# A four-layer decoder trunk on one core: the state-space layers' small matmuls in four quarters of the array, two copies pinned, fetches moved and one order rewritten

## The chip, the core and the metric

The kernel runs on one core of a Trainium2 chip. The metric is the device time of one execution in microseconds (us). A core has TensorE (PE in the profile, PEld for its weight loads), VectorE (DVE), ScalarE (ACT), GpSimd (POOL) and SyncE (SP), which run side by side and wait for one another by semaphores. SP, ACT and POOL also issue DMAs, each in its own order, so that an instruction waiting at the head of a queue holds up what stands behind it.

## What is computed

A decoder trunk of four layers over 256 positions with 1024 features. Each layer has a token mixer, an MLP with squared ReLU and a gated input per layer ("ple"). The mixers of layers 0 and 3 are S5, a diagonal complex state-space model; layer 1 has forgetting attention, layer 2 gated linear attention. The change touches S5 alone. Cut to what matters:

```python
u = xn @ w_in                                  # (256, 1024): 64 groups of 16 channels
ab = exp((lam_re + 1j * lam_im) * dt)          # per group, 64 states
x = einsum('bsgc,gnc->bsgn', u, bbar)          # into the states, complex
s = associative_scan(s_t = ab * s_(t-1) + x_t) # over time
y = real(einsum('bsgn,gcn->bsgc', s, c)) + d_skip * u
z1, z2 = split(gelu(y) @ w_glu)
out = (z1 * sigmoid(z2)) @ w_out
```

## The kernel before

The residual stream lies in SBUF as features by time, float32. Large matrix products split each float32 weight tile into a high and a low part (`parts`: ACT casts the high part, L182; DVE subtracts for the low part, L184) and run three matmuls per pair of tiles (L201 to L203, or `wide`, L237 and L239). S5's small products are plain float32 matmuls, each of which is two records in the trace.

S5 takes time in steps of four positions, so that one group has 4 x 16 = 64 inputs and outputs per step, 64 steps and 64 states. The 64 groups are worked in four blocks b of 16: eight pairs p, and in a pair the halves g = 0 (partitions 0 to 63) and g = 1 (64 to 127). One block goes through these steps, each a letter in an order string:

- w: projection `x @ w_in` in eight pieces, two per block (L1241); D: the DMA of a piece's weights on SP.
- u: scale by the norm, and eight small DMAs on SP and ACT that turn the block's inputs into U, 64 inputs by 64 steps per group (L1247, L1075).
- i, r, o, k (layer 0 only): DVE builds the weights into the states, the rotations, the weights out of them and the direct part tm (L968 to L993, L1008 to L1045). For layer 3 the same things are computed during earlier MLPs (`s5_ahead`) and kept in DRAM ("kept").
- f, q (in layer 3): fetch from DRAM, on POOL: f takes win (weights in) and rot, q the weights out and tm (L1215, L1052).
- x: `s5_way_in`, matmuls from U to the states (L1087), one per pair, half, and real or imaginary part, and twice that in layer 0, where each weight comes in two terms. Results lie in two PSUM tiles "wk", the real and the imaginary one.
- s: `s5_states` on DVE: rotation (L1097 to L1099) and the scan (L1102). e: `s5_turned`, rotation back (L1110 to L1121).
- y: `s5_outputs`, matmuls from U and the states to the outputs in one PSUM tile "mk" (L1133), then a GELU on ACT (L1142).
- t: four transposes on PE into the PSUM tile "po" (L1149) and a copy of the high part (L1150); g: its low part on DVE (L1313).
- a, b: gate products of w_glu's second half, one unit of a block's features each (L201 to L203); d: DMA of such a unit; l: its split. P, p: the ple projection's DMA and its pieces (L470).
- c, n, z: the norm.

In x and y each matmul has 64 rows by 64 columns of weights and 64 moving columns. Half g reads partitions of its half and writes partitions of the same half, so the two matmuls of a pair lie on the diagonal of the 128 x 128 array.

The order strings FIRST (layer 0) and LATER (layer 3) say in which order steps are written down. A scheduler then orders each engine's instructions, by that order and its own model of time; in layer 3 `in_order` holds PE to the written order. `issue_after(i)` puts an engine's instructions behind instruction i of the same engine. Tiles come from pools by tag, with as many buffers as BUFS says, and a tile waits until its buffer's last user is done. "win" has one buffer, shared with scratch of `s5_in`; "wt" has four, "po" and "mk" one each, "raw" three.

Of the kernel before, what the change touches and what calls it, by code (L numbers as in the profile page):

```python
# [22 lines left out]
        "acc": 3, "wk": 3, "po": 1, "mk": 1}  # L23
# [6 lines left out]
LATER = """D0 D2 D1 D3 c0 w0 w2 n0 z0 f0 q0 w1 z1 D4 D5 u0 w3 P0 u1 w4 D6 D7 d0 x0 s0 w5 d1 f1 q1 x1 e0 w6 y0 u2 s1 w7 t0 l0 g0 f2 x2 u3 P1 e1 q2 y1 l1 d2  # L30
s2 p0 p1 t1 g1 f3 x3 q3 p2 e2 y2 p3 d3 s3 a0 t2 g2 l2 d4 b0 l3 d5 a1 e3 l4 d6 b1 l5 d7 y3 a2 l6 t3 b2 l7 g3 a3 b3"""
# [29 lines left out]
class Trunk:  # L61
# [849 lines left out]
    def s5_table(self, j, F):  # L911

        nc = self.nc
        ps = self.psum((128, 2, 128), "mk")
        nc.tensor.matmul(ps.rearrange("p i x -> p (i x)"), self.zero[:, 0:128], self.zero[:, 0:256], start=True, stop=True)
        for i in range(2):
            nc.tensor.transpose(ps[:, i, :], F[:, i].rearrange("x s p -> x (s p)"), self.ident)
        ct = self.a2("ct", (128, 2, 2, 64))
        nc.scalar.copy(ct.rearrange("x i g n -> x i (g n)"), ps)
        self.ct = ct  # L920
        tab = self.dram.tile([2, 4, 4, 2, 8, 64], F32, name=f"tab{j}")
        for i in range(2):
            for g in range(2):
                nc.gpsimd.dma_start(tab[g, :, :, i].rearrange("s b p n -> (s b) p n"), ct[:, i, g, :])
        return tab

    def s5_spread(self, b):

        out = []
        for i in range(2):  # L930
            ps = self.psum()
            for p in range(8):
                for g in range(2):
                    self.last_mm = self.nc.tensor.matmul(ps[g * 64:(g + 1) * 64, p * 64:(p + 1) * 64], self.pick[:, p], self.ct[:, i, g, :], start=True, stop=True, skip_group_check=True)
            out.append(ps)
        return out
# [8 lines left out]
    def s5_fetch_in(self, j, b, pin=lambda x: x):  # L945
        bT = self.t4("bT", (128, 2, 512), tag="wt")
        pin(self.nc.gpsimd.dma_start(bT, self.A["s5_bT"][j, b]))
        return bT

    def s5_fetch_powers(self, tab, b, pin=lambda x: x):  # L950
        cf = self.t4("coef", (128, 2, 512), tag="wt")
        for g in range(2):
            pin(self.nc.gpsimd.dma_start(cf[g * 64:(g + 1) * 64], tab[g, :, b].rearrange("s i p n -> s (i p n)").unsqueeze(0).broadcast_to([16, 4, 1024])))
        return cf
# [6 lines left out]
    def s5_in(self, b, bT, cf, ahead=False):  # L961

        nc = self.nc
        if not ahead:
            w = [self.wp.tile([128, 2, 8, 64], F32, name=n, tag=n, bufs=BUFS[n]) for n in ("wh", "wl")]
            f = [t.rearrange("x i p n -> x i (p n)") for t in w]
            re, im = cf
            nc.vector.tensor_tensor(f[0], bT, re.unsqueeze(1).broadcast_to([128, 2, 512]), ALU.mult)  # L968
# [4 lines left out]
        w = [self.flat(win[:, i]) for i in range(2)]  # L973
        t = self.scratch((2, 512))
        t = [t[:, i] for i in range(2)]
        self.two(w[0], bT[:, 0], cf[:, 0], bT[:, 1], cf[:, 1], ALU.subtract, t[0])
        yield
        self.two(w[1], bT[:, 0], cf[:, 1], bT[:, 1], cf[:, 0], ALU.add, t[1])
        self.keep(b, 0, win, ahead)
# [97 lines left out]

    def s5_way_in(self, U, win):

        xs = []  # L1080
        for ri in range(2):
            px = self.psum((128, 8, 64))
            for p in range(8):
                for i, w in enumerate(win[ri]):
                    for g in range(2):
                        r = slice(g * 64, (g + 1) * 64)
                        self.nc.tensor.matmul(px[r, p, :], w[r, p], U[r, p, :], start=i == 0, stop=i == len(win[ri]) - 1, skip_group_check=True)  # L1087
            xs.append(px)
        return xs

    def s5_states(self, xs, rot, d0):
# [3 lines left out]
        X, Y = (t.rearrange("x i p j -> x (i p j)").rearrange("x (p i j) -> x p i j", p=8, i=2) for t in (P, W))  # L1095
        for t, px in zip((X, Y), xs):
            V.tensor_tensor(t, px.unsqueeze(2).broadcast_to([128, 8, 2, 64]), rot, ALU.mult)  # L1097
        V.tensor_tensor(R[:, 0], X[:, :, 1], Y[:, :, 0], ALU.add)
        V.tensor_tensor(R[:, 1], X[:, :, 0], Y[:, :, 1], ALU.subtract)  # L1099
# [24 lines left out]
    def s5_outputs(self, U, terms, out, tm):  # L1124
# [3 lines left out]
        py = self.psum((128, 8, 64), "mk")  # L1128
        gs = [slice(g * 64, (g + 1) * 64) for g in range(2)]
        def add(x, w, start=False, stop=False):  # L1130
            for p in range(8):
                for g in range(2):
                    nc.tensor.matmul(py[gs[g], p, :], x[gs[g], p, :], w[gs[g], :, p] if w is not tm else w[gs[g], p], start=start and p == 0,  # L1133
                                     stop=stop and p == 7, skip_group_check=True)


        add(U, tm, start=True)
        parts = [(t[n], out[i]) for n in range(len(terms[0])) for i, t in enumerate(terms)]
        for n, (t, w) in enumerate(parts):
            add(t, w, stop=n == len(parts) - 1)  # L1140
        G = self.t2("G", (128, 4, 8, 16))
        self.last_gelu = nc.scalar.activation(G, py.rearrange("x p (i c) -> x i p c", i=4), AF.Gelu_apprx_tanh)  # L1142
# [57 lines left out]
    def s5_start(self, l):  # L1200
# [100 lines left out]
        def e(b):  # L1301
            states[b] = self.s5_turned(*states[b], rots[b][0], first)
# [41 lines left out]
        steps = dict(D=D, w=w, u=u, c=c, n=n, z=z, f=f, j=j_, q=q_, r=r, i=i, o=o, k=k, x=x_, s=s, e=e, y=y, t=t, g=g, P=P, p=p, d=d, l=ahead, a=lambda b: gate(0, b),  # L1344
# [144 lines left out]
def layout(inputs):  # L1489
# [42 lines left out]
```

## Time and profile before

| | |
|---|---|
| median of 3 runs | 1417.9 us (1415.36 to 1418.76) |
| profiled execution | 1413.62 us, its span 1411.9 us |
| mean granted TensorE clock | 0.994 |
| layer 0's S5, x of block 0 to g of block 3 | 29.96 to 123.6 us |
| layer 3's S5, w of piece 0 to g of block 3 | 1058.03 to 1137.8 us |
| ACT busy over the span | 708.5 us (50%) |
| DMA | 254.80 MB, mean 180 GB/s |

The span runs from the first to the last instruction; the execution's own time lies a little around it. A row of the timeline has the start, the length, engine, line, operation, the tile written and those read, the shape and the count of merged records; in brackets how long the engine was idle before and what ended that. A row of busy time by stage has the window and its length, busy us and records of PE, PEld, DVE, ACT and POOL, the granted TensorE clock, the DMA share and GB/s.

### The profile page before, as it was taken

How to read it: one execution, taken by the hardware profiler on the slowest of the kernel's cores; microseconds unless marked ns; L12 is line 12 of the kernel's file. 1: busy time of each engine (PE TensorE's matmuls, PEld its weight loads, DVE VectorE, ACT ScalarE, POOL GpSimd, SP SyncE). 2: the span in 40 equal slices, each digit the busy share in tenths (PEclk: the TensorE clock that was granted, in tenths of full speed). 3: DMA queues.
4: the chain of work that ended last, by engine and by line, in shares of the span. 5: the costliest groups of instructions: out<-in, count | busy, mean ns of one | idle time of the engine just before them, and what ended most of it. 6: DMA issues, size and time to landing. Idle time of an engine off the chain costs nothing.

```text
span 1411.9 us, 26657 instructions
## 1 busy us (share of the span) xinstructions
PE 1376.1 (97%) x10794; PEld 1247.5 (88%) x10794; DVE 1034.7 (73%) x1638; ACT 708.5 (50%) x1110; POOL 107.7 (8%) x179
## 2 busy tenths in 40 slices
PE   9898999999999999999999999999999999999997
PEld 8788988889999978888988698888998899888897
DVE  9985678776867678897676568888666857766764
ACT  3234565454645565455566355555452355545553
POOL 3000000010110000110005100100004100000020
PEclk9999999999999999999999999999999999999999
DMA  9434656657554446776665356666666455556551
GB/s 306 128 114 124 182 176 196 184 182 234 181 149 138 133 136 209 249 232 206 183 187 148 107 162 195 212 206 220 203 207 204 164 195 172 187 167 212 188 180 60
DMA packets 144475, 254.80 MB, mean 180 GB/s; under 512 B 22192, under 2 KB 33552, under 8 KB 144352
## 3 DMA queue, kind: packets, MB, share of 16 engines
q1 hardware_dynamic: 130336, 227.80, 51.9%
q0 software_dynamic: 7744, 23.73, 4.9%
q10 hardware_dynamic: 6272, 1.58, 0.5%
q8 instruction: 84, 1.38, 0.4%
q14 instruction: 39, 0.32, 0.1%
HBM read 242.81 MB, written 8.13 MB: 178 GB/s over the span
## 4 chain that ended last, share of the span: by engine, by line
PE 65%; ACT 1%; DVE 1%; issue 1%; POOL 1%; DMA 1%; DVEq 0%; POOLq 0%; ACTq 0%; SPq 0%
PE wk L237 9%; PE acc L237 7%; PE wk L239 5%; PE acc L239 4%; PE acc L201 3%; PE wk L201 3%; PE wk L202 3%; PE wk L203 3%; PE acc L202 3%; PE acc L203 3%; PE mk L237 3%; PE po L237 2%; PE acc L1241 2%; PE mk L239 1%; PE acc L264 1%; PE acc L265 1%
## 5 line engine op out<-in xcount | busy, mean ns | idle before, releaser
L184 DVE TENSOR_TENSOR wlo<-raw,whi 128x1024 fp32r<-128x1024 f32 x396 | 482.5, 1226 | 270.5 <-ACT whi L182 266.2
L182 ACT CAST whi<-raw 128x1024 fp32r<-128x1024 f32 x396 | 412.5, 1049 | 484.3 <-PE po L237 73.8
L237 PE MATMUL wk<-x,whi 128*128 128x512 f32 x576 | 181.7, 396 | 0.8 <-DVE relu L248 0.8
L239 PEld LDWEIGHTS wk<-x,wlo 128*128 128x128 f32 x576 | 107.1, 188 | 23.6
L237 PE MATMUL acc<-s,whi 128*128 128x512 f32 x384 | 119.7, 395 | 0.0
L239 PE MATMUL wk<-x,wlo 128*128 128x256 f32 x576 | 113.4, 279 | 0.0
L237 PEld LDWEIGHTS wk<-x,whi 128*128 128x128 f32 x576 | 89.8, 189 | 2.5 <-DVE relu L248 0.8
L239 PEld LDWEIGHTS acc<-s,wlo 128*128 128x128 f32 x384 | 71.4, 188 | 16.5
L201 PE MATMUL acc<-x,whi 128*128 128x256 f32 x288 | 81.6, 287 | 0.9 <-ACT pp L456 0.9
L203 PE MATMUL acc<-x,wlo 128*128 128x256 f32 x288 | 82.1, 286 | 0.2 <-DVE wlo L184 0.2
L202 PE MATMUL acc<-x,whi 128*128 128x256 f32 x288 | 81.8, 285 | 0.0
L237 PE MATMUL mk<-x,whi 128*128 128x512 f32 x256 | 81.6, 395 | 0.0
L239 PE MATMUL acc<-s,wlo 128*128 128x256 f32 x384 | 76.0, 280 | 0.0
L203 PE MATMUL wk<-s,wlo 128*128 128x256 f32 x256 | 72.4, 283 | 0.0
L202 PE MATMUL wk<-s,whi 128*128 128x256 f32 x256 | 72.4, 283 | 0.0
L201 PE MATMUL wk<-s,whi 128*128 128x256 f32 x256 | 72.4, 283 | 0.0
L237 PE MATMUL po<-s,whi 128*128 128x512 f32 x192 | 60.3, 395 | 0.0
L237 PE MATMUL wk<-s,whi 128*128 128x512 f32 x192 | 59.5, 395 | 0.0
L237 PEld LDWEIGHTS acc<-s,whi 128*128 128x128 f32 x384 | 58.9, 189 | 0.6
L237 PE MATMUL acc<-x,whi 128*128 128x512 f32 x192 | 58.8, 396 | 0.0
L239 PEld LDWEIGHTS mk<-x,wlo 128*128 128x128 f32 x256 | 47.6, 188 | 10.3
L201 PEld LDWEIGHTS acc<-x,whi 128*128 128x128 f32 x288 | 54.7, 191 | 1.9 <-ACT pp L456 1.1
(413 smaller groups left out, 3382.6 us busy)
## 6 DMA issues: line engine op xcount, KB each, us to landing
raw<-mlp_w SPq DMA_DIRECT2D x256, 512.0 KB, 3.8
raw<-s_w_glu SPq DMA_DIRECT2D x32, 512.0 KB, 4.5
raw<-ple_gate SPq DMA_DIRECT2D x32, 512.0 KB, 3.6
raw<-fox_w_in SPq DMA_DIRECT2D x24, 512.0 KB, 3.8
raw<-gla_w_in SPq DMA_DIRECT2D x24, 512.0 KB, 3.7
raw<-s_w_out SPq DMA_DIRECT2D x16, 512.0 KB, 3.6
kept<-kept POOLq DMA_DIRECT2D x12, 512.0 KB, 5.3
raw<-ple_proj SPq DMA_DIRECT2D x8, 512.0 KB
```

Of the source, the lines that this page charges most:

```text
L182: nc.scalar.copy(hi, raw)
L184: self.last_lo = nc.vector.tensor_tensor(lo, raw, hi.bitcast(F32), ALU.subtract)
L201: mm(ps, hi, x[:, 0], start=first, stop=False, skip_group_check=True)
L202: mm(ps, hi, x[:, 1], start=False, stop=False, skip_group_check=True)
L203: self.last_mm = mm(ps, lo, x[:, 0], start=False, stop=last, skip_group_check=True)
L237: mm(ps[n], hi[:, i, s], v[i], start=first and i == 0, stop=False, skip_group_check=True)
L239: self.last_mm = mm(ps[n][:, 0], lo[:, i, s], v[i][:, 0], start=False, stop=last and i == UK - 1, skip_group_check=True)
L264: mm(ps[half], a[:, 0, t], hi[:, k], start=k0 + k == 0, stop=False)
L265: mm(ps[half], a[:, 0, t], lo[:, k], start=False, stop=False)
L1241: self.last_mm = nc.tensor.matmul(ps[:, n], raw[:, k, c], x[4 * i + k], start=i == k == n == 0, stop=i == 1 and k == 3, skip_group_check=True)
```

## The change

- In pairs p = 4 to 7 the two groups trade halves where states lie: the state of half g lies on partitions of half 1 - g. The host lays out lam, b, c and d so (`turned`), and the table of powers is stored by h = p // 4. With that a step of x or y has four matmuls in a row, h = 0 and 1 by g = 0 and 1, one in each 64 x 64 quarter of the array: those of h = 1 lie off the diagonal.
- x writes PSUM tiles by h, not by real and imaginary part; y writes two half-sized tiles, "mk" for h = 0 and "po" for h = 1. Matmuls are as many as before, of the same size.
- s works on one h at a time: two products of the old size, four adds of half the old size. The GELU comes in two halves.
- For y's direct term with h = 1 the inputs must lie on the other half of the partitions: `s5_inputs_turned` copies U's pairs 4 to 7 across, two ACT copies per block, in step e, and for b > 0 pinned behind the last GELU written down.
- Layer 3: win is fetched by a step of its own, F, into "wt", no longer by f into "win". The order LATER is new: F0 and F1 near the norm, F2 and F3 after w4; u2 ahead of e0; step v7 is w7 with t0 between its halves; x3 ahead of t1 and p1; a0 ahead of y2; p2, p3 after y2; g1 after y2, g2 after a1.
- Powers are fetched by four DMAs per block on POOL, not two.

```diff
+        "v1": 2, "acc": 3, "wk": 3, "po": 1, "mk": 1}
-LATER = """D0 D2 D1 D3 c0 w0 w2 n0 z0 f0 q0 w1 z1 D4 D5 u0 w3 P0 u1 w4 D6 D7 d0 x0 s0 w5 d1 f1 q1 x1 e0 w6 y0 u2 s1 w7 t0 l0 g0 f2 x2 u3 P1 e1 q2 y1 l1 d2
-s2 p0 p1 t1 g1 f3 x3 q3 p2 e2 y2 p3 d3 s3 a0 t2 g2 l2 d4 b0 l3 d5 a1 e3 l4 d6 b1 l5 d7 y3 a2 l6 t3 b2 l7 g3 a3 b3"""
+LATER = """D0 D2 D1 D3 c0 w0 w2 n0 F0 z0 f0 q0 F1 w1 z1 D4 D5 u0 w3 P0 u1 w4 F2 F3 D6 D7 d0 x0 s0 w5 d1 f1 q1 x1 u2 e0 w6 y0 s1 v7 f2 x2 u3 l0 g0 P1 e1 q2 y1 l1 d2
+s2 p0 f3 x3 t1 p1 q3 a0 e2 y2 p2 d3 g1 s3 l2 p3 t2 d4 b0 l3 d5 a1 g2 e3 l4 d6 b1 l5 d7 y3 a2 l6 t3 b2 l7 g3 a3 b3"""
...
+        for g in range(2):
+            for h in range(2):
+                pin(self.nc.gpsimd.dma_start(cf[g * 64:(g + 1) * 64, h].rearrange("x i k -> x (i k)"),
+                                             tab[g ^ h, :, b, h].rearrange("s i p n -> s (i p n)").unsqueeze(0).broadcast_to([16, 4, 512])))
...
+    def s5_inputs_turned(self, U):
+
+        V = self.t2("V", (128, 4, 64), tag="v1")
+        for g in range(2):
+            self.nc.scalar.copy(V[g * 64:(g + 1) * 64], U[(1 - g) * 64:(2 - g) * 64, 4:8])
+        return U, V
...
     def s5_way_in(self, U, win):
-        xs = []
+        xs = [self.psum((128, 2, 4, 64)) for _ in range(2)]
+        gs = [slice(g * 64, (g + 1) * 64) for g in range(2)]
         for ri in range(2):
-            px = self.psum((128, 8, 64))
-            for p in range(8):
+            for p in range(4):
                 for i, w in enumerate(win[ri]):
-                    for g in range(2):
-                        r = slice(g * 64, (g + 1) * 64)
-                        self.nc.tensor.matmul(px[r, p, :], w[r, p], U[r, p, :], start=i == 0, stop=i == len(win[ri]) - 1, skip_group_check=True)
-            xs.append(px)
+                    for h in range(2):
+                        for g in range(2):
+                            self.nc.tensor.matmul(xs[h][gs[g ^ h], ri, p], w[gs[g], 4 * h + p], U[gs[g], 4 * h + p], start=i == 0,
+                                                  stop=i == len(win[ri]) - 1, skip_group_check=True)
         return xs
     def s5_states(self, xs, rot, d0):
-        X, Y = (t.rearrange("x i p j -> x (i p j)").rearrange("x (p i j) -> x p i j", p=8, i=2) for t in (P, W))
-        for t, px in zip((X, Y), xs):
-            V.tensor_tensor(t, px.unsqueeze(2).broadcast_to([128, 8, 2, 64]), rot, ALU.mult)
-        V.tensor_tensor(R[:, 0], X[:, :, 1], Y[:, :, 0], ALU.add)
-        V.tensor_tensor(R[:, 1], X[:, :, 0], Y[:, :, 1], ALU.subtract)
+        for h, (t, px) in enumerate(zip((P, W), xs)):
+            p = slice(4 * h, 4 * h + 4)
+            t = self.flat(t).rearrange("x (r p i j) -> x r p i j", r=2, p=4, i=2)
+            V.tensor_tensor(t, px.unsqueeze(3).broadcast_to([128, 2, 4, 2, 64]), rot[:, p].unsqueeze(1).broadcast_to([128, 2, 4, 2, 64]), ALU.mult)
+            V.tensor_tensor(R[:, 0, p], t[:, 0, :, 1], t[:, 1, :, 0], ALU.add)
+            V.tensor_tensor(R[:, 1, p], t[:, 0, :, 0], t[:, 1, :, 1], ALU.subtract)
...
-        py = self.psum((128, 8, 64), "mk")
+        py = [self.psum((128, 4, 64), tag) for tag in ("mk", "po")]
...
+        for n in range(-1, len(parts)):
+            for p in range(4):
+                for h in range(2):
+                    for g in range(2):
+                        q, r = 4 * h + p, gs[g ^ h]
+                        x, w = (us[h][r, p], tm[r, q]) if n < 0 else (parts[n][0][r, q], parts[n][1][r, :, q])
+                        nc.tensor.matmul(py[h][gs[g], p, :], x, w, start=n < 0 and p == 0, stop=n + 1 == len(parts) and p == 3, skip_group_check=True)
...
+        for h in range(2):
+            self.last_gelu = nc.scalar.activation(G[:, :, 4 * h:4 * h + 4], py[h].rearrange("x p (i c) -> x i p c", i=4), AF.Gelu_apprx_tanh)
...
-                win = fetch(b, 0, (128, 2, 8, 64), "win")
-                ins[b] = [[win[:, i]] for i in range(2)]
...
+        def F(b):
+            win = fetch(b, 0, (128, 2, 8, 64), "wt")
+            ins[b] = [[win[:, i]] for i in range(2)]
...
         def e(b):
+            with self.tc.issue_after(self.last_gelu.ins) if b else nullcontext():
+                us[b] = self.s5_inputs_turned(us[b])
             states[b] = self.s5_turned(*states[b], rots[b][0], first)
```

More of the change, by code (lines that the diff above doesn't have):

```diff
@@ L933, in s5_spread @@
                 for g in range(2):
-                    self.last_mm = self.nc.tensor.matmul(ps[g * 64:(g + 1) * 64, p * 64:(p + 1) * 64], self.pick[:, p], self.ct[:, i, g, :], start=True, stop=True, skip_group_check=True)
-            out.append(ps)
+                    self.last_mm = self.nc.tensor.matmul(ps[g * 64:(g + 1) * 64, p * 64:(p + 1) * 64], self.pick[:, p], self.ct[:, i, g ^ (p > 3), :], start=True, stop=True, skip_group_check=True)
+            out.append(ps.rearrange("x (h k) -> x h k", h=2))
         return out
@@ L947, in s5_fetch_in @@
         pin(self.nc.gpsimd.dma_start(bT, self.A["s5_bT"][j, b]))
-        return bT
+        return bT.rearrange("x i (h k) -> x i h k", h=2)
     def s5_fetch_powers(self, tab, b, pin=lambda x: x):
-        cf = self.t4("coef", (128, 2, 512), tag="wt")
+        cf = self.t4("coef", (128, 2, 2, 256), tag="wt")
         for g in range(2):
-            pin(self.nc.gpsimd.dma_start(cf[g * 64:(g + 1) * 64], tab[g, :, b].rearrange("s i p n -> s (i p n)").unsqueeze(0).broadcast_to([16, 4, 1024])))
-        return cf
+            for h in range(2):
+                pin(self.nc.gpsimd.dma_start(cf[g * 64:(g + 1) * 64, h].rearrange("x i k -> x (i k)"),
+                                             tab[g ^ h, :, b, h].rearrange("s i p n -> s (i p n)").unsqueeze(0).broadcast_to([16, 4, 512])))
+        return [cf[:, :, i] for i in range(2)]
     def s5_fetch_out(self, j, b, pin=lambda x: x):
@@ L972, in s5_in @@
         win = self.t4("win", (128, 2, 8, 64), tag="c4")
-        w = [self.flat(win[:, i]) for i in range(2)]
-        t = self.scratch((2, 512))
+        w = [win[:, i].rearrange("x (h p) n -> x h (p n)", h=2) for i in range(2)]
+        t = self.scratch((2, 2, 256))
         t = [t[:, i] for i in range(2)]
-        self.two(w[0], bT[:, 0], cf[:, 0], bT[:, 1], cf[:, 1], ALU.subtract, t[0])
+        self.two(w[0], bT[:, 0], cf[0], bT[:, 1], cf[1], ALU.subtract, t[0])
         yield
-        self.two(w[1], bT[:, 0], cf[:, 1], bT[:, 1], cf[:, 0], ALU.add, t[1])
+        self.two(w[1], bT[:, 0], cf[1], bT[:, 1], cf[0], ALU.add, t[1])
         self.keep(b, 0, win, ahead)
@@ L1122, in s5_turned, with s5_outputs @@
         return [[P[:, 0]], [P[:, 1]]]
-    def s5_outputs(self, U, terms, out, tm):
+    def s5_outputs(self, us, terms, out, tm):
         nc = self.nc
-        py = self.psum((128, 8, 64), "mk")
+        py = [self.psum((128, 4, 64), tag) for tag in ("mk", "po")]
         gs = [slice(g * 64, (g + 1) * 64) for g in range(2)]
[L1130 to L1137, printed above, removed]
-        parts = [(t[n], out[i]) for n in range(len(terms[0])) for i, t in enumerate(terms)]
-        for n, (t, w) in enumerate(parts):
-            add(t, w, stop=n == len(parts) - 1)
+        parts = [(t[n], out[i]) for n in range(len(terms[0])) for i, t in enumerate(terms)]
+        for n in range(-1, len(parts)):
[5 more added lines that the diff above has]
+                        nc.tensor.matmul(py[h][gs[g], p, :], x, w, start=n < 0 and p == 0, stop=n + 1 == len(parts) and p == 3, skip_group_check=True)
         G = self.t2("G", (128, 4, 8, 16))
-        self.last_gelu = nc.scalar.activation(G, py.rearrange("x p (i c) -> x i p c", i=4), AF.Gelu_apprx_tanh)
+        for h in range(2):
+            self.last_gelu = nc.scalar.activation(G[:, :, 4 * h:4 * h + 4], py[h].rearrange("x p (i c) -> x i p c", i=4), AF.Gelu_apprx_tanh)
         return G
@@ L1269, in f @@
                 cf = self.s5_fetch_powers(self.tab, b, self.tc.keep_in_program_order) if b else None
-                parts[b] = bT, [cf[:, i] for i in range(2)] if b else self.s5_spread(b)
+                parts[b] = bT, cf if b else self.s5_spread(b)
             else:
-                win = fetch(b, 0, (128, 2, 8, 64), "win")
-                ins[b] = [[win[:, i]] for i in range(2)]
                 rots[b] = fetch(b, 1, (128, 8, 2, 64), "m4"), decay(b)
+        def F(b):
+            win = fetch(b, 0, (128, 2, 8, 64), "wt")
+            ins[b] = [[win[:, i]] for i in range(2)]
         def j_(b):
@@ L1342, in gate @@
                 self.sg.append(sg)
-        steps = dict(D=D, w=w, u=u, c=c, n=n, z=z, f=f, j=j_, q=q_, r=r, i=i, o=o, k=k, x=x_, s=s, e=e, y=y, t=t, g=g, P=P, p=p, d=d, l=ahead, a=lambda b: gate(0, b),
+        steps = dict(F=F, v=lambda i: w(i, lambda: t(0)), D=D, w=w, u=u, c=c, n=n, z=z, f=f, j=j_, q=q_, r=r, i=i, o=o, k=k, x=x_, s=s, e=e, y=y, t=t, g=g, P=P, p=p, d=d, l=ahead, a=lambda b: gate(0, b),
                      b=lambda b: gate(1, b))
```

22 lines of the change are left out of this document (13 added, 9 removed).

## The prediction

> **What bounds the kernel now.** I read the page first, then the stages in which the changed lines run: busy time by stage, the lines' own instructions, the timelines of PE, DVE and POOL, last the waits.
>
> ```profile
> PE 1376.1 (97%) x10794; PEld 1247.5 (88%) x10794; DVE 1034.7 (73%) x1638; ACT 708.5 (50%) x1110; POOL 107.7 (8%) x179
> ```
> ```profile
> 20.00:115.00 95.00, 86.62 (x1500) 78.77 (x1500) 87.58 (x103) 25.97 (x53) 7.62 (x16) 0.98 0.50 151
> 1077.00:1122.00 45.00, 41.68 (x669) 37.11 (x666) 43.20 (x51) 12.32 (x20) 11.80 (x21) 1.00 0.59 193
> ```
>
> Over the span PE is the bound (97%, DVE 73%). In the two S5 stages the columns PE, PEld, DVE, ACT, POOL say otherwise: in 45 us of layer 3 DVE is busy 43.20 and PE 41.68; in 95 us of layer 0, 87.58 against 86.62. Two engines are full at once there, and work taken from PE is worth only what DVE lets through.
>
> The matmuls that the change packs, first and last of three groups, then of four:
>
> ```profile
> L1087 PE MATMUL wk<-U,wh x256: 218/218/267, 30.0 to 105.5; 64*64 64x64 f32 x128
> ...
> L1087 PE MATMUL wk<-U,kept x256: 218/218/267, 1076.7 to 1110.6; 64*64 64x64 f32 x128
> L1133 PE MATMUL mk<-tm,U x256: 218/218/267, 48.7 to 1130.4; 64*64 64x64 f32 x128
> ...
> L1133 PE MATMUL mk<-kept,P x256: 218/218/219, 1091.3 to 1132.3; 64*64 64x64 f32 x128
> ```
>
> That is 7 x 256 = 1792 records, two to a matmul. By the code's loops a block has 128 + 160 records in layer 0 and 64 + 96 in layer 3, so 1152 and 640.
>
> ```profile
> 1076.72 2.08 PE L1087 MATMUL wk<-U,kept 64*64 64x64 f32 x64
> ...
> 1084.65 2.08 PE L1087 MATMUL wk<-U,kept 64*64 64x64 f32 x64 [2.20 <-issue]
> 1086.67 3.72 PE L1241 MATMUL acc<-x,raw 128*128 128x256 f32 x16
> 1090.32 1.15 PE L1133 MATMUL mk<-tm,U 64*64 64x64 f32 x32
> ...
> 1101.74 1.10 PE L1133 MATMUL mk<-tm,U 64*64 64x64 f32 x32
> ...
> 1110.73 1.99 PE L470 MATMUL wk<-praw,raw 128*128 128x256 f32 x8
> 1112.66 1.15 PE L1133 MATMUL mk<-tm,U 64*64 64x64 f32 x32
> ...
> 1117.25 0.47 PE L201 MATMUL acc<-g,whi 128*128 128x256 f32 x1
> ...
> 1120.31 0.60 PE L1149 MATMUL po<-ident,G 128*128 128x128 f32 x4
> ```
>
> Sixty-four records start over 2.08 us less the last one's 0.218: 29.6 ns from start to start, a round of two quarters (g = 0, 1) in 59 ns. A projection step (w, L1241) takes 3.65 us (1086.67 to 1090.32), a ple piece (p) 1.93, a gate 3.06 (1117.25 to 1120.31), a turn (t) 0.60.
>
> **The quarters.** Each round now has four matmuls, one per quarter of the array. Three rows bound a round of four:
>
> ```profile
> 61.81 0.65 PE L1033 MATMUL mk<-qo,bx 128*32 128x64 f32 x32
> 785.69 0.48 PE L702 MATMUL mk<-v,ku 64*128 64x256 f32 x1
> 785.70 0.48 PE L702 MATMUL po<-v,ku 64*128 64x256 f32 x1
> ```
>
> L1033 runs four column strips with the same 64 moving columns: (0.65 - 0.22)/31 = 13.9 ns per record, its last record lasting as long as the others above. So PE can start four in a round. L702 starts a matmul on each half of the rows at once, over all columns, into two banks: the pairing that is new here (the change puts h = 0 and h = 1 into two PSUM tiles). No row shows four 64x64 loads in a round, so the price lies between 13.9 and 29.6 ns; I take 14.8, half, since every pairing in it is seen to overlap. On PE that is 1792 x 14.8 = 26.5 us: 17.0 in layer 0, 9.5 in layer 3.
>
> The Trainium skill (TensorE: Matmul & The Clock Gate, "Wait — 56ns, not 53.3ns?") says that start-to-start never drops below about 25 ns, however small the matmul. By that the saving would be 1792 x 4.6 = 8.2 us of PE at most, an estimate from that page. This trace disagrees: L1033 goes at 13.9 ns, and the measurement decides.
>
> **Layer 3, walked through.** PE's order is written out; DVE's chain is u, s, e for each block.
>
> ```profile
> 1077.91 1.23 DVE L1097 TENSOR_TENSOR P<-wk,kept 128x1024 f32<-128x1024 f32 x1 [3.49 <-PE wk L1087]
> ...
> 1095.39 1.04 DVE L1247 TENSOR_TENSOR u<-acc,rstd 128x512 f32<-128x512 f32 x1
> ...
> 1099.94 0.69 DVE L1313 TENSOR_TENSOR g<-po,g 128x512 fp32r<-128x512 f32 x1 [0.33 <-ACT g L1150]
> 1101.02 1.23 DVE L1097 TENSOR_TENSOR P<-wk,kept 128x1024 f32<-128x1024 f32 x1 [0.39 <-PE wk L1087]
> ...
> 1103.41 0.69 DVE L1098 TENSOR_TENSOR R<-P,W 128x512 f32<-128x512 f32 x1
> ...
> 1110.54 1.22 DVE L184 TENSOR_TENSOR wlo<-raw,whi 128x1024 fp32r<-128x1024 f32 x1
> ```
>
> Block 2's s and e ran without a break from 1101.02 to 1110.54: 9.5 us. The change cuts the two half-sized adds of s into four: at most 2 x (2 x 0.69 - 1.23) = 0.3 us more; I take 0.15, as ends overlap, so 9.7. The start of s doesn't move: it began 1.2 us after x0, when the first of two PSUM tiles was full; now both are full after the halved 1.0 us.
> - y0: DVE has s0, u2 (moved ahead, 1.0) and e0 = 10.7 from 1077.91, so y0 starts at 1088.6, 1.7 earlier than 1090.32. PE has x0, w5, x1, w6 = 9.3 from 1076.72 and waits some 2.6 us.
> - y1: s1, e1, u3, g0 and perhaps a weight split (1.2) = 11.4 to 12.6: 1100.0 to 1101.2, against 1101.74. PE has y0, w7, t0, x2 = 6.8 and waits 4.6 to 5.8 us.
> - y2: s2, e2, g1 and a split = 11.6: 1111.6 to 1112.8, against 1112.66: nothing to 1.1 us gained.
> - After y2 PE is the bound. Before: y2 2.9, p 1.9, a0 3.1. Now: y2 1.5, two p 3.9, since a0 ran earlier; and y3 is 1.5 shorter. That is 7.9 - 5.4 + 1.5 = 4.0. The third split may hold b1 by 1 us.
>
> Sum for layer 3: 0.5 + 4.0, that is 4.5 us (3 to 6), not the 9.5 + 2.2 that PE alone would give.
>
> Where the 2.2 us went:
>
> ```profile
> 1079.11 1.64 POOL L1215 DMA_DIRECT2D kept<-kept  x3 [8.26 <-PE wk L1087]
> ...
> kept<-kept POOLq DMA_DIRECT2D x12, 512.0 KB, 5.3
> ```
>
> The one "win" buffer held the fetch of block 1's win until x0 had read it; with 5.3 us to land it came at about 1084.4, when x1 began. Step F fetches all four into free "wt" buffers ahead. F is four issues of 0.55 us on POOL, as many as f had; F0 passes the rstd's power step on POOL, which has w1's 3.6 us as cover; were that gone, 0.55. Behind the old wait stood block 1's rot and tm fetches, which come earlier too. U2's copies pass v7 and s1; on SP they stand behind the fetch d1, which frees with w6, at about 1086: landed before x2.
>
> **Layer 0.** PE's order there is the scheduler's, so I count the waits.
>
> ```profile
> 52.65 2.95 PE L1133 MATMUL mk<-qo,P 64*64 64x64 f32 x64 [2.10 <-DVE P L1112]
> ...
> 116.08 1.15 PE L1133 MATMUL mk<-tm,U 64*64 64x64 f32 x32 [0.62 <-DMA tm<-lags]
> ...
> 118.90 2.06 PE L1133 MATMUL mk<-qo,W 64*64 64x64 f32 x64
> ```
> ```profile
> L184 DVE TENSOR_TENSOR wlo<-raw,whi 128x1024 fp32r<-128x1024 f32 x8 | 9.8, 1219 | 3.9 <-ACT whi L182 3.9
> ...
> L1008 DVE TENSOR_TENSOR qo<-bc,cpow 128x1280 f32<-128x1280 f32 x4 | 5.9, 1486 | 1.7 <-PE mk L1133 1.7
> ...
> L1097 DVE TENSOR_TENSOR W<-wk,rot 128x1024 f32<-128x1024 f32 x4 | 4.9, 1220 | 1.1 <-PE wk L1087 1.1
> ```
> ```profile
> 122.96 0.69 DVE L1313 TENSOR_TENSOR g<-po,g 128x512 fp32r<-128x512 f32 x1 [8.49 <-ACT g L1150]
> ```
>
> DVE's idle time up to 115 us is 7.4. Of it 1.7 + 1.1 waits for the packed matmuls themselves and goes; 3.9 waits for weight casts whose buffers a gate frees, behind a y or x in PE's queue: I count a third, 1.3. After e3 DVE waits 8.49 us for y3, GELU, turn and copy: y3 (116.08 to 120.96) loses half, 2.4. Against it: 4 x 0.15 for s, 0.1 for the GELU in two. Sum 1.7 + 1.1 + 1.3 + 2.4 - 0.6 - 0.1 = 5.8; I take 5.5 (2.4, the tail alone, to 9).
>
> **Costed at nothing.** V, two copies of half the partitions per block, is new on ACT:
>
> ```profile
> 1069.92 0.37 ACT L377 COPY rstd<-wk 128x256 f32<-128x256 f32 x1 [5.60 <-PE wk L375]
> ```
>
> Eight of at most 0.37 us are 3 us per layer; ACT had 26 of 95 and 12 of 45 us busy. A copy waits for the GELU of the block before; weight casts and ple copies queue behind it, but that GELU is long done when e(b) comes; without cover it is 0.7 per block before y. Powers come in four DMAs: six more issues in layer 0, 3.3 us of a POOL busy 7.6 of 95. y(b) now needs the PSUM tag "po" free of the turn of b - 1, so waits for g(b - 1): in the new order y2 stands ahead of g1, behind p1 and a0 (5.0 us of cover); that g1 is in the sum for y2.
>
> Total 4.5 + 5.5 = 10.0 us. The profiled run took 1413.6, so 1403.6; the median of the runs shown is 1417.9, and 1417.9 x 1403.6/1413.6 gives 1408. From the worked ends (5.4 to 15 us less) it would be 1403 to 1413.
>
> **Rivals.**
> (A) PE sets the end after all: DVE's steps fall into PE's shadow, and the whole 26.5 + 2.2 comes through: 1389. Against it: 43.20 of 45 us. Chance 0.07.
> (B) The packing doesn't do what it says: the two quarters of one row half take turns, or a matmul's two records go back to back, and a round of four takes two of 59 ns. PE saves nothing, s costs 1.2 us, the fetch gives up to 2.2: about 1417. For it: no row has four 64x64 loads in a round. Against: L702 and L1033. Chance 0.16. The Trainium skill (TensorE: Matmul & The Clock Gate, "The mechanism") has a rule on this side: weight loads overlap running matmuls only where the row group differs, and here two loads per round share one. The trace leans against it: no room for a load after its matmul is seen in the 59 ns round.
> (C) Slower: writes of two row halves into one column strip, small as these are, drain between, and a round costs more than two rounds of two. Each ns per record is 1.8 us. With 2.2 left to gain, slower by 0.3% (4.3 us, about what a measurement of this kernel tells from no change) starts at 29.6 + 6.5/1.79 = 33.2 ns, a round of 133. Four in a row would be 59 ns per record and +53 us: 1470. Against it: L702. Chance 0.06.
> (D) The new waits of PE bring a slow clock:
>
> ```profile
> 49.80:53.20 3.40, 1.30 (x43) 1.16 (x40) 3.40 (x6) 0.00 (x0) 0.00 (x0) 1.00 0.74 203
> 53.20:56.60 3.40, 3.40 (x78) 3.40 (x74) 2.34 (x2) 2.33 (x2) 0.00 (x0) 0.55 0.02 8
> ```
>
> After 3.4 us with 1.30 busy the granted clock was 0.55 for the next 3.4, which costs up to 1.5 us. The waits before y0, y1, y2 and as many in layer 0 could do the same, partly under DVE's shadow: three or four take 5 us: 1413. Chance 0.13.
>
> **How the numbers follow.** The forecast has 0.58. Faster: 0.55 of it, A's 0.07, two thirds of D and a little of B: 0.73. Same: the rest of D, most of B and a little of the forecast: 0.19. Slower: C and a little of B: 0.08. The range 1398 to 1417 leaves out A, C and the outer tails.
>
> **What would show it.** Right: L1087 and L1133 at about 15 ns per record; the 2.20 wait before x1 gone; PE idle before y0 and y1 in layer 3, ended by DVE; DVE over 95% busy from x0 to e3. Wrong: 25 ns or more per record (B, C); waits before y that end on a GELU, a V copy or g; or y1 much before 1100.

## The result, and the profile after

After: 1422.6 us (median of 17 runs) against 1417.8 us before (17 runs): ratio 1.0028, 95% interval 1.0018 to 1.0038. The forecast was 10 us less; the change took some 4 more. The profiled run of after took 1419.4 us (span 1416.6).

First the page's busy times and the two stages (columns as before: PE, PEld, DVE, ACT, POOL, clock, DMA share, GB/s), first layer 0, then the 18 us around the first x of layer 3:

```profile
PE 1360.3 (96%) x10794; PEld 1229.4 (87%) x10794; DVE 1035.8 (73%) x1654; ACT 715.3 (50%) x1134; POOL 113.9 (8%) x193
```
```profile
20.00:115.00 95.00, 78.19 (x1496) 68.74 (x1497) 88.52 (x111) 29.39 (x64) 10.69 (x22) 0.93 0.52 153
1064.00:1082.00 18.00, 12.89 (x114) 11.10 (x113) 2.93 (x5) 0.99 (x3) 12.28 (x22) 0.89 0.92 313
```

PE is busy 15.8 us less, and 8.4 less in layer 0, while DVE fills as much of that window as before (88.5 us). In layer 3 the DMA share is 0.92; before, the like stretch had 0.63:

```profile
1066.00:1084.00 18.00, 16.45 (x130) 14.05 (x129) 8.80 (x13) 2.49 (x4) 8.61 (x15) 1.00 0.63 194
```

Now the timelines of after: PE at x0, DVE at s0, POOL's issues ahead of them, and the chain of waits.

```profile
1076.14 0.33 PE L1096 MATMUL wk<-U,kept 64*64 64x64 f32 x4 [1.67 <-DMA U<-u]
1079.91 1.97 PE L1096 MATMUL wk<-U,kept 64*64 64x64 f32 x60 [3.44 <-DMA U<-u]
```
```profile
1081.74 1.23 DVE L1107 TENSOR_TENSOR P<-wk,kept 128x1024 f32<-128x1024 f32 x1 [9.63 <-PE wk L1096]
```
```profile
1058.29 0.57 POOL L1224 DMA_DIRECT2D kept<-kept  x1
1063.85 0.71 POOL L365 TENSOR_TENSOR rrow<-rrow,mhalf 128x2 f32<-128x2 f32 x1 [4.99 <-DVE rrow L361]
1064.54 1.12 POOL L1224 DMA_DIRECT2D kept<-kept  x2
1065.64 2.31 POOL L1054 DMA_DIRECT2D tm<-kept  x4
1067.94 1.61 POOL L1224 DMA_DIRECT2D kept<-kept  x3
1070.09 1.04 POOL L1224 DMA_DIRECT2D kept<-kept  x2 [0.53 <-DMA tm<-kept]
1071.12 1.71 POOL L1054 DMA_DIRECT2D tm<-kept  x3
```
```profile
1069.09 0.64 SPq L1077
...
1069.78 2.01 SPq L1077
...
1071.85 7.93 DMA U<-u
```

Before, x0 stood at 1076.72 without a wait, and POOL waited 8.26 us there for x0 to free the win buffer. Now no buffer stops POOL: F0 goes at 1058.29, well ahead, but F1 to F3 and block 1's rot and weights out, 512 KB each, are issued from 1067.9 to 1071.1, just ahead of and among U0's eight small copies (from 1069.09 on), and the copy that x0's second part waits for lands 7.93 us after its issue. x0 starts in two parts, s0 at 1081.74 where it stood at 1077.91, though layer 3 itself began 2.3 us earlier.

Where PE doesn't wait first, the quarters do what was forecast. In a_hold (an experiment below), where x0 has no wait, its 64 records start over 0.95 us (15.0 ns from start to start); in before they took 29.6:

```profile
L1096 PE MATMUL wk<-U,kept x64: 218/218/267, 1075.4 to 1076.3; 64*64 64x64 f32 x64
```

In layer 0 the forecast's last term came as it was sized: DVE's wait before the last g fell from 8.49 to 6.15 us.

```profile
120.53 0.69 DVE L1326 TENSOR_TENSOR g<-po,g 128x512 fp32r<-128x512 f32 x1 [6.15 <-ACT g L1159]
```
```profile
L184 DVE TENSOR_TENSOR wlo<-raw,whi 128x1024 fp32r<-128x1024 f32 x8 | 9.8, 1220 | 5.4 <-ACT whi L182 5.4
...
L1010 DVE TENSOR_TENSOR qo<-bc,cpow 128x1280 f32<-128x1280 f32 x4 | 5.9, 1484 | 0.0
...
L1107 DVE TENSOR_TENSOR W<-wk,rot 128x1024 f32<-128x1024 f32 x4 | 4.9, 1216 | 0.0
```

The waits for the packed matmuls (1.7 and 1.1) are gone; the one for weight casts grew from 3.9 to 5.4.

### The profile page after: what moved, and what is told of

It reads as the page before. It is cut to its first block, busy times and chain, and to the rows that moved or that the text cites. A ratio compares the mean times of both kernels' runs of the same rounds, so it can differ in the third digit from the quotient of the medians.

```text
span 1416.6 us, 26735 instructions
## 1 busy us (share of the span) xinstructions
PE 1360.3 (96%) x10794; PEld 1229.4 (87%) x10794; DVE 1035.8 (73%) x1654; ACT 715.3 (50%) x1134; POOL 113.9 (8%) x193
## 4 chain that ended last, share of the span: by engine, by line
PE 61%; DVE 4%; ACT 2%; DMA 1%; issue 1%; POOL 1%; SPq 0%; DVEq 0%; POOLq 0%; ACTq 0%
PE wk L237 9%; PE acc L237 7%; PE wk L239 5%; PE acc L239 4%; PE wk L201 3%; PE wk L202 3%; PE wk L203 3%; PE acc L201 3%; PE acc L202 3%; PE acc L203 3%; PE mk L237 3%; PE po L237 2%; PE mk L239 1%; PE acc L264 1%; PE acc L265 1%; PE acc L266 1%
```

## The experiments

T1, the theory: the 512 KB fetches, no longer held back, fill the DMA engines while U0's copies must land, and the chain of DVE behind x0 shifts as a whole. T2, the rival: the new order of layer 3 is the loss. This table takes times from every kernel's one profile (us); the ratio is that of the medians of all runs. w0: first projection of layer 3; s0: first product of s; e3: end of the last e; MLP: first matmul of the MLP behind the stage; end: of the span.

```
kernel       w0       w0-s0  s0-e3  e3-MLP  MLP-end   ratio to before (95%)
before       1058.03  19.88  43.95  68.67   221.37
b_same       1059.13  19.88  44.69  69.10   221.38    (one run)
after        1055.71  26.02  44.24  68.11   222.54    1.0028 (1.0018 to 1.0038)
a_same       1054.17  26.85  44.21  68.63   222.48    (one run)
a_hold       1056.68  19.88  45.60  68.40   222.49    0.9982 (0.9971 to 0.9992)
b_early      1059.55  25.63  48.32  69.98   221.34    1.0052 (1.0037 to 1.0067)
a_oldorder   1057.07  19.88  44.91  66.14   222.49    0.9960 (0.9945 to 0.9975)
a_two        1057.87  19.88  43.96  68.21   222.51    0.9974 (0.9965 to 0.9983)
a_old2       1055.41  19.88  47.04  65.93   222.52    0.9977 (0.9967 to 0.9987)
a_small      1059.56  21.82  43.96  67.78   222.51    (one run)
a_drain      1056.37  19.92  44.91  66.06   220.21    0.9945 (0.9933 to 0.9957)
a_drain2     1062.23  19.88  44.91  66.11   218.91    0.9974 (0.9965 to 0.9984)
a_pairs      1059.33  20.00  44.95  68.12   222.52    0.9996 (0.9987 to 1.0006)
b_dve        1061.59  19.88  49.05  65.94   221.39    1.0022 (1.0012 to 1.0033)
a_dve        1058.19  19.92  51.19  63.11   222.53    1.0022 (1.0011 to 1.0034)
a_two_raw4   1057.26  19.93  43.97  66.57   222.56    0.9958 (0.9945 to 0.9970)
b_neworder   1062.79  19.88  43.94  73.55   221.37    1.0031 (1.0016 to 1.0046)
a_best       1056.95  19.94  44.93  65.45   220.29    0.9938 (0.9925 to 0.9951)
```

**a_hold: the fetch undone.** In after, each F step goes back to directly before f, and its tag:

```
-            win = fetch(b, 0, (128, 2, 8, 64), "wt")
+            win = fetch(b, 0, (128, 2, 8, 64), "win")
```

> The kernel after, with one thing undone: the kept win of a block is fetched into the one win buffer again, right before that block's rot and tm, so that x0 holds POOL's fetches back as it did before. Quarters, V copies and the rest of the new order stay. T1 (the fetches moved ahead fill the DMA engines while the eight small U0 copies must land, x0 starts 24.2 us after w0 instead of 18.7, and the DVE-bound chain behind x0 shifts by as much): x0 comes back to 18.7 to 19.5 us after w0, the DMA share between 1064 and 1082 us to about 0.65, and the end 4 to 6 us earlier than the kernel after, ratio to before 0.998 to 1.000. x1 pays the old wait for its win, at most 2.2 us, out of DVE's shadow. T2 (the loss is in the new order of layer 3: y1 behind g0 for the shared po, GELUs behind U issues): x0 comes back, but the end stays within 1 us of the kernel after, ratio 1.002 to 1.004.

x0 is back at 18.7 us after w0, s0 at 19.88 instead of 26.02, the DMA share between 1064 and 1082 us at 0.61, and the kernel 0.46% (6.5 us) faster than after, a little more than expected. T1 holds. The wait before x1 was 2.72 us, more than the 2.2 expected.

**b_early: the fetch alone.** In before, the steps F0 to F3 at the places of the change, into wt.

> The kernel before, with one thing of the change alone: the kept win is fetched by a step of its own, at the places of the change, into the four wt buffers. Halves, tags and the rest of the order are those of before. T1 (the fetches delay U0's copies): x0 starts 23 to 25 us after w0 instead of 18.7, and the kernel is slower by 3 to 5.5 us, ratio 1.002 to 1.004. T2 (the new order or the shared po is the loss, the fetch is harmless): the wait of 2.2 us before x1 goes and the kernel is the same to 2.2 us faster, ratio 0.9985 to 1.000.

s0 late by 5.75 us and the kernel 0.52% slower, more than expected. U2's copies were late too: block 3's fetches went out just ahead of them, from 1103.86 on (in before from 1102.21 on, behind x2), and x2 waited 5.91 us. T2's reading of the fetch as harmless falls.

```profile
1080.39 0.45 PE L1087 MATMUL wk<-U,kept 64*64 64x64 f32 x8 [2.08 <-DMA U<-u]
...
1110.06 3.68 PE L1087 MATMUL wk<-U,kept 64*64 64x64 f32 x64 [5.91 <-DMA U<-u]
```

**a_small: bytes or issues.** In after, F fetches 128 of 1024 columns, and POOL zeroes the rest.

```
-            win = fetch(b, 0, (128, 2, 8, 64), "wt")
+            nc.gpsimd.memset(f[:, 128:], 0.0)
+            nc.gpsimd.dma_start(f[:, :128], self.kept[0][b, 0, :, :128])
```

> The kernel after, but F fetches only the first 128 of the 1024 columns of each kept win (64 KB instead of 512 KB) and POOL sets the rest to zero, so the S5 weights of layer 3 are left out in seven eighths; the issues and their places are those of the change. T1 (the bytes in front of U0's copies on the DMA engines are the cost): x0 starts 18.7 to 20.5 us after w0, all of its records together, and the DMA share from 1064 to 1082 us falls from 0.92 to about 0.7. T1b (the cost is the issues or their order on POOL, whatever their size): x0's second part stays at 23 to 25 us after w0.

x0's second part starts 20.9 us after w0, s0 21.82: 4.2 of the 6.1 us are back with the same issues in the same places, so most of it is bytes. That is one run, and short of what T1 expected: x0 still came in two parts, the second later than 20.5. The 1.9 left (the copy that x0's second part waited for took 4.85 us here) go with block 1's rot, weights out and tm, which still ran unheld; that part was not tried by itself.

**a_oldorder and a_two.** a_oldorder is after with the old order and the old fetch; a_two is after with F0 and F1 ahead of n0, F2 and F3 behind x0 and x2:

```
+            win = fetch(b, 0, (128, 2, 8, 64), "wt" if b % 2 else "win")
```

> The kernel after with the whole old order of the later layers and the old fetch of win; quarters, halves in two PSUM tiles and V copies stay, in both layers. T1: x0 at about 18.7 us after w0, layer 0's 2.4 us kept, and in layer 3 the PE work after the last e (y3 and what is left of y2) shorter by 1.5 to 3: 2 to 5 us faster than before, ratio 0.9965 to 0.9985; against the fetch held back in the new order the difference is within 2 us. T2: the new order itself costs 4 to 5 us, so this kernel beats the new order with the old fetch by that much, ratio to before 0.995 to 0.998 while the other stays at 1.002 to 1.004. A third cause, that V's copies or the GELU in halves cost what the quarters save: same as before, 0.9995 to 1.002.

> The kernel after with the fetches in other places: the kept wins of blocks 0 and 1 before the step that takes the inverse root (n0), so some 3 us earlier than F0 and F1 in the change, and those of blocks 2 and 3 behind x0 and x2, in the buffer that they free. T1: the 512 KB fetches are over or held back when U0's copies go, x0 at 18.7 to 20 us after w0 and x1 without a wait for its win: 5 to 7 us faster than the kernel after, ratio to before 0.997 to 0.9995. T2: within 1 us of the kernel after, 1.002 to 1.004.

Both keep s0 at 19.88. a_two is 7.6 us (0.54%) under after: the fetch can go early, if it is over when the copies go. But the old order beats the new one (held fetch) by 0.22%, 3 us, with intervals that just overlap: T1 explains why after is slower than before, and T2 has a part of its own, 2.3 us of it behind e3. The third cause falls: with V's copies and the GELU in halves a_oldorder is 0.4% faster than before.

**b_neworder: the order alone,** in before, without F.

> The kernel before with one part of the change alone: the new order of the later layers, without the steps F (the wins are fetched as before), the quarters, V and the second PSUM tag. With the quarters and the fetches held, the new order took 3.0 us more from w0 to the MLP of layer 3 than the old one (133.9 against 130.9), 2.3 of it after the last e. T7 (the order itself costs that, by the weight pieces that come later behind the last e): from w0 to the MLP 134 to 136 us instead of 132.5, ratio 1.001 to 1.0025. T8 (it costs only together with the shared PSUM tag or the quarters): 131 to 133, ratio 0.999 to 1.0005.

The order alone costs, so T8 falls: 137.4 us from w0 to the MLP against 132.5 and 133.7, all of it behind e3, more than T7 gave it, at a ratio of 1.0031 (1.0016 to 1.0046). T7's reason, the weight pieces, isn't in the trace: behind x3 PE doesn't wait once up to the MLP. It lost the time at x3, before e3, and carried it along. The rows of PE's stretch around x3, in b_neworder and in before:

```profile
1106.00:1118.00 12.00, 9.14 (x141) 7.53 (x137) 11.09 (x14) 2.74 (x5) 3.34 (x6) 0.76 0.71 228
```
```profile
1103.00:1115.00 12.00, 12.00 (x232) 10.74 (x228) 11.90 (x15) 4.39 (x8) 3.15 (x6) 1.00 0.61 204
```

Between y1 and x3 the old order has p0, p1 and t1 (in before 3.56 and 0.53 us), which cover U3's copies; the new one has p0 alone. x3 waited 1.25 us for its own win, which the one win buffer had held back, and 1.43 more for U3's copies. PE stood for 2.9 of 12 us, and the granted clock was 0.76 in the stretch (before: busy throughout, at 1.00). In a_hold the same x3 waited longer, and there too PE had no wait behind it up to the MLP:

```profile
1106.67 0.48 PE L1096 MATMUL wk<-U,kept 64*64 64x64 f32 x4 [5.24 <-DMA U<-u]
1108.01 1.98 PE L1096 MATMUL wk<-U,kept 64*64 64x64 f32 x60 [0.86 <-DMA U<-u]
```

That isn't all that the new order costs. In a_two x3 doesn't wait, and from e3 to the MLP it takes 68.21 us all the same, where a_oldorder takes 66.14; with a fourth raw buffer (a_two_raw4, below) 1.6 us of it goes.

**a_old2: early fetch in the old order.** a_two's fetch places in a_oldorder.

> The kernel with the quarters and the old order (the one that took 0.996 of before), and its win fetches moved: blocks 0 and 1 before n0, 2 and 3 behind x0 and x2, alternating between the win buffer and a wt buffer. T1 (large fetches must be over or held when U0's copies go; DVE sets s0 to e3): x0 stays at 18.7 us after w0, the wait of 1.8 us before x1 goes, s0 to e3 falls from 44.9 back to about 44.0 us, and the kernel is 0 to 1.5 us faster than with the old fetch: ratio 0.995 to 0.996. A rival, that any fetch started ahead delays U0's copies: x0 late by 2 us or more and the kernel slower than 0.998.

A miss: x0 and x1 were as expected, but x2 waited 2.97, 0.85 and 2.40 us for U2's copies (2.71 and 0.86 in a_oldorder), and s0 to e3 became 47.0. At 1094.39 POOL issued a 512 KB fetch of block 3, with block 3's four tm fetches behind it; U2's copies went at 1092 to 1094. In a_oldorder block 3's fetches came at 1099.44, held until x2 had freed the win buffer, and so behind U2's copies. That is T1 once more, two blocks further on, but holding back this one fetch was not tried by itself. POOL's rows in a_old2 and in a_oldorder, then a_old2's chain:

```profile
1094.39 0.55 POOL L1224 DMA_DIRECT2D kept<-kept  x1 [6.56 <-DVE W L1129]
```
```profile
1099.44 1.64 POOL L1224 DMA_DIRECT2D kept<-kept  x3 [11.33 <-PE wk L1096]
```
```profile
1094.15 4.54 DMA U<-u
...
1098.73 1.17 PE wk L1096 x32
```

**a_pairs: two quarters at a time.** In a_oldorder the loop over h goes outside that over p.

> The kernel with the quarters and the old order, with one thing undone: the loop over the two halves h stands outside that over p, so that a round has two matmuls on a diagonal pair of quarters, as many as before the change. V copies, two PSUM tiles, GELU halves and the fetches stay. This prices the concurrency of four by itself. T1 (DVE sets the S5 stages up to the last e, so that PE's halved time buys only layer 0's y3 and at most y3 of layer 3): records at about 29.6 ns, PE busy 17 + 9.5 us more, but the kernel only 3 to 6 us slower than with four quarters: ratio to before 0.998 to 1.0005. T2 (PE was a bound through the stages, and the gain was lost to the fetches alone): slower by 12 us or more, ratio over 1.004.

Slower by 0.36% (5 us), but no clean test: PE interleaved the two halves in part, records in layer 3 came at 20.4 ns in y and 21.4 in x0, not 29.6, and PE was busy 10.7 us more, not 26.5. About half of what PE lost showed in the time.

**b_dve and a_dve: a DVE product doubled,** in before and in a_oldorder:

```
         V.tensor_tensor(P[:, :, :, 1:64], r, c.unsqueeze(1).broadcast_to([128, 2, 8, 63]), ALU.mult)
+        V.tensor_tensor(P[:, :, :, 1:64], r, c.unsqueeze(1).broadcast_to([128, 2, 8, 63]), ALU.mult)
```

> The kernel before, with one VectorE instruction per S5 block doubled: e's first product (P from R and the cosines, 1.2 us) is issued twice, in layer 0 and in layer 3, eight instructions and 9.6 us of DVE in all. T1 (DVE sets the end of the S5 stages, before the change already): the kernel is slower by 7 to 10 us, ratio 1.005 to 1.007. T2 (PE set the end and DVE had slack): slower by less than 3 us, ratio under 1.002.

> The same doubling of e's first product in the kernel with the quarters and the old order. T1: DVE is as much the bound as before, so it pays the full 9.6 us, 8 to 10 us over the 0.996 of that kernel: ratio 1.0015 to 1.003. T2 (PE was the bound and only now DVE is): the same here, but with less than 3 us in the kernel before. So the two together tell whether PE's saving met a DVE bound that was there already: of equal costs, DVE was the bound before; a cost here that is larger by x us says that PE held x us of it before.

Of 9.6 us more DVE work before pays 0.22% (3.1 us, 1.7 to 4.7); the kernel with quarters pays 0.62% (8.8). With the doubled product the two kernels are equally fast, 1.0022 both. So T1, as put here, falls for before: by the expectation's own rule PE held some 5.7 us (give or take 3) over what DVE alone would have taken, and that is all that a_oldorder gained (0.4%, 5.7 us). Read so, the quarters took PE down to DVE's time, and there the gain stops. In layer 3 both kernels pay the delay in full up to e3 (49.05 and 51.19) and get about half of it back behind e3; from w0 to the MLP they pay 2.4 and 3.3. The rest of the difference must lie ahead of layer 3, which the one profile of each (w0 at 1061.6 and 1058.2) doesn't show: a_dve's profiled run is 4.1 us under its median.

**a_drain and a_drain2: POOL's last DRAIN.** The quarters' kernels end 1.14 us later behind the MLP (222.5 against 221.4). There the trace has a DRAIN on POOL, and the other engines' last semaphores come right behind it: 8.90 us in before, 10.04 in after. In a_oldorder the powers go to SP, in a_drain2 the fetches of bT and bc too:

```
-                pin(self.nc.gpsimd.dma_start(cf[g * 64:(g + 1) * 64, h]...
+                pin(self.nc.sync.dma_start(cf[g * 64:(g + 1) * 64, h]...
```

> The kernel with the quarters and the old order, with one thing changed: the coefficient powers (28 of POOL's 113 DMAs) are issued on SP. In the profiles POOL's last DRAIN takes 8.90 us with 99 POOL DMAs and 10.04 us with 113, 81 ns for each of the 14 more, and the end waits for it. T1d (the drain grows with the number of DMAs that POOL issued): 85 DMAs give a drain of 10.04 - 28 x 0.081 = 7.8 us and the kernel ends 2.3 us sooner after its last matmul, 8.1 instead of 10.4 us. T2d (the drain is set by something else of the change, as the packets or the output's writes): it stays at 10.0 us. The time as a whole also feels what SP's queue does with the new DMAs in layer 0 (0 to 3 us more): ratio 0.9945 to 0.998.

> The kernel with the quarters, the old order and the powers issued on SP, and besides them the fetches of bT and bc (16 DMAs) on SP: POOL issues 69 DMAs. T1d: its last drain takes 0.84 + 69 x 0.0814 = 6.5 us instead of 7.8, and the end comes 1.3 us sooner after the last matmul, if what SP does after the output's write (done 5.6 us after the last matmul) doesn't set it first. The time as a whole: 0 to 1.5 us under that kernel's 0.9945, unless SP's queue in layer 0 suffers from the new fetches (then up to 3 us over it).

The longest of POOL's three last DRAINs (the third duration, in ns) in before, after, a_drain and a_drain2:

```profile
L1528 POOLq DRAIN  x3: 40/93/8898, 1402.2 to 1411.6; - x3
```
```profile
L1550 POOLq DRAIN  x3: 40/102/10042, 1405.8 to 1416.4; - x3
```
```profile
L1550 POOLq DRAIN  x3: 40/93/7762, 1398.9 to 1407.2; - x3
```
```profile
L1550 POOLq DRAIN  x3: 40/93/6455, 1404.8 to 1411.8; - x3
```

```
kernel      DMAs issued on POOL   last DRAIN, us
before       99                    8.90
after       113                   10.04
a_drain      85                    7.76
a_drain2     69                    6.46
```

81 ns for each DMA, on a line through all four: T1d holds. a_drain's ratio is 0.15% (2.1 us) under a_oldorder's, with intervals that overlap; in a_drain2 the end came another 1.3 us sooner, but the kernel was 0.29% (4 us) slower than a_drain, more than the 3 us allowed, and w0 was at 1062.2. That reads as SP's queue in layer 0 taking back more than the end gave, and was not tried by itself.

**a_two_raw4 and a_best: the weight pieces.** Four raw buffers, three wt (`"raw": 4`, `"wt": 3`), in a_two and in a_drain.

> The kernel with the quarters, the new order and the wins of blocks 0 and 1 fetched early (0.9974), with four raw buffers for the weight pieces instead of three; the wt buffers are three instead of four to make room, which bears on layer 0 alone. T3 (after the last e the end hangs on the loop of weight pieces: DVE's second half frees a raw buffer, a DMA of 4 to 5 us fills it, ACT casts, DVE takes the other half; that is why PE's halved y3 and the moved a0 bring nothing behind y2): from e3's end to the MLP 68.2 us becomes 65.5 to 67, with PE's waits of 1.6, 0.8 and 0.3 us for weights gone, and layer 3 is 1 to 2.7 us shorter. T4 (something else holds PE there, as the order of its own work): 68.2 within 0.5 us.

> Candidate for the fastest: the quarters, the old order with the old fetch, the powers issued on SP (0.9945 so far), and four raw buffers for weight pieces with three wt buffers. T3 (behind the last e the loop of weight pieces holds the end, in the old order too, where DVE waited 2.95, 2.13 and 1.93 us for it): from e3's end to the MLP 64.7 to 65.6 us instead of 66.1, ratio 0.993 to 0.9945. If PE was full there already in the old order: no change from 0.9945.

The chain behind e3 in a_two, which three raw buffers make:

```profile
1121.71 1.15 DVE wlo L184
1122.88 4.27 DMA raw<-s_w_glu
1127.17 1.05 ACT whi L182
1128.25 1.24 DVE wlo L184
1129.50 3.81 DMA raw<-s_w_glu
1133.39 1.06 ACT whi L182
```

e3 to the MLP falls by 1.6 us in the new order, where PE's waits there go from 1.60 us (for the low part of a weight), 0.78 and 0.34 (for g of block 3, not for weights, as the expectation has it) to one of 1.18 for a weight, and by 0.6 in the old one: T3 holds for that much. a_best has the lowest ratio, 0.9938 of before, within the interval of a_drain.

**b_same and a_same: second profiles.**

> The kernel before once more, unchanged, for a second profile of it: its first one is 4.2 us under the median of its runs. Open: how much of the change's time lies ahead of layer 3. Profiles of kernels with the quarters have layer 3's first projection (w0) at 1055.4 to 1059.6 us, 1057.0 on average; the first profile of before has it at 1058.0. T5 (layer 0 gains 5 us, as forecast): w0 here at 1061 to 1063. T6 (layer 0 gains only the 2.4 us of its last block): w0 at 1058 to 1060. Layer 3 from w0 to the end within 0.5 us of 353.9 in both.

> The kernel after once more, unchanged, for a second profile: the first took 1419.4 where the median of its runs is 1422.6. Under T1 the delay of U0's copies by the fetches varies from run to run: x0's last part starts 23 to 28 us after w0, and from w0 to the end it is 360 to 364 us where before has 353.9. If T5 holds (layer 0 gains 5 us), its median asks for about 363.

b_same's w0 (1059.1) lies in T6's band, so T5 is not borne out by it; its time from w0 to the end was 355.0 us, 1.2 over the 353.9 and not within 0.5 of it. But one profile's w0 says little, as w0 spreads over some 5 us between profiles. Over the four profiles with layer 0 as before (before, b_same, b_early, b_neworder) the mean is 1059.9; over the seven with the change's layer 0 and nothing else ahead of layer 3 (after, a_same, a_hold, a_small, a_two, a_oldorder, a_old2) it is 1056.6. That is 3.2 us, give or take 2.5 (two standard errors). a_same's s0 was later still, its w0 to the end 362.2 us.

## Why the prediction was wrong

By pieces, from means over both profiles of each kernel: s0 6.6 us later (26.4 against 19.9), s0 to e3 0.1 less, e3 to the MLP 0.5 less, the end 1.1 more; and 3.2 less ahead of layer 3, from the eleven profiles above: +3.9 us. Measured: 0.28%, 4.0 us. The 3.2 is known to 2.5 us only, so that the two agree this closely is luck.

- **The step that failed:** "The start of s doesn't move", and with it the price of F. The prediction counted F as "four issues of 0.55 us on POOL" and took it as a plus that "behind the old wait stood block 1's rot and tm fetches, which come earlier too". The wait on the win buffer was also a brake that kept 512 KB fetches off the DMA engines until x0 had its inputs. Without it s0 came 6 to 7 us later. Undone alone it gave 6.5 us back, done alone it cost 7.4, and with the F fetches cut to an eighth of their bytes 4.2 of s0's 6.1 us came back. The prediction had the DMA share of the stage in hand (0.59) and asked when U2's copies would land, never when U0's would.
- **The new order.** The forecast had 4.0 us behind y2, since "After y2 PE is the bound". It was 0.5 in after and 2.5 with the old order. The step took PE to be without waits there. In a_hold x3, which had lost its cover, waited 6.1 us for U3's copies; in a_two x3 didn't wait, but PE waited 1.60 us for a weight piece. In after x3 waited 2.7 us. How much of after's shortfall goes to each was not worked out. The order alone costs before 0.31%.
- **The quarters:** right as a price per round. Records at 15.0 ns in a_hold's x0 and 14.8 in its y0 against 14.8 taken; a round of four starts takes the 59 ns that a round of two took. Rivals B and C are out. But PE's busy time fell by 15.8 us where 26.5 were forecast: the sum priced every record at full clock, and behind a wait they came further apart (x0's last 60 records took 1.97 us in after, all 64 take 1.16 in a_hold; the granted clock from 1076 to 1082 us was 0.67 in after). The Trainium skill (TensorE: Matmul & The Clock Gate, "Wait — 56ns, not 53.3ns?") has 25 ns as the least from start to start; these runs disagree with it (15.0 and 14.8), as L1033 did (13.9).
- **Layer 0:** the tail's 2.4 us as sized (8.49 to 6.15). The other terms went into the wait for weight casts in part; 3.2 us in all by profiles, where 5.5 were forecast and 2.4 was the low end.
- **DVE as the bound of layer 3:** right. s0 to e3 is 44 us in before, after and a_two alike, and in b_dve the doubled product shows there in full. All but the first four records of y1 waited 3.5 us for g0 in after, one of the signs that the prediction gave for being wrong: up to e3 PE's wait for the shared "po" cost nothing; whether it costs behind e3 was not tried. No wait of PE before y in layer 3 ended on a V copy or a GELU. But the 0.5 us that s0 to e3 was to gain didn't come, and behind e3 half of b_dve's delay came back. Rival A is out.
- **Rival D** took part: the granted clock from 20 to 115 us, in layer 0, was 0.93 and 0.95 in the two profiles of after (0.98 and 0.96 in those of before), and over all profiles 0.89 to 0.96 with the quarters, 0.96 to 0.99 without. What that cost was not tried by itself. Not every wait did it: behind x1 the next projection took 3.65 us in before (a wait of 2.20) and in b_neworder (3.11), but 5.71 in a_hold (2.72):

```profile
1085.00:1091.00 6.00, 6.00 (x40) 4.73 (x44) 6.00 (x11) 0.69 (x1) 3.95 (x7) 0.66 0.88 274
```

- **Not in the sum:** POOL's last DRAIN, 1.1 us. The prediction counted six more DMAs on POOL, those of layer 0; there are fourteen (L953 14, now L954 28), as `s5_ahead` fetches powers for layer 3's four blocks too.

Open: the gain ahead of layer 3 more closely than 1 to 6 us, what held the last 1.9 us of U0's copies in a_small, and why some of PE's waits bring a low clock and others don't.

## What to carry to other kernels

A wait on a buffer can be the only thing that keeps a large transfer from small ones on which the critical chain hangs: before taking it away, list what it holds back, in bytes, and what must land in that time. Work that is reordered loses its cover as well: for each transfer, ask what stands between its issue and its user in the new order. And when two engines are both nearly full, price the relief of one by doubling a piece of the other.

## What was not expected of the hardware

- The end of these kernels waits for a DRAIN on POOL whose time grew by 81 ns with every DMA that POOL had issued in the whole kernel (6.46 us at 69, 7.76 at 85, 8.90 at 99, 10.04 at 113). Issuing 28 of them elsewhere took 2.3 us off the end.
- One of U0's eight small copies took 7.93 us to land beside 512 KB fetches (the like one 4.85 when the F fetches were cut to 64 KB).
- Four 64x64 quarters run in a round of 59 to 60 ns, as long as a round of two (14.8 and 15.0 ns per record against 29.6), where no wait went ahead.
